# Layer 0's z, q and k products as seven block products for eight, ahead of the SSD branch

## The chip, the core and the metric

One core of a Trainium2 chip runs the whole step. Its engines work side by side, each in the order of its own instructions: PE (TensorE) multiplies and accumulates into PSUM, DVE (VectorE) and ACT (ScalarE) do element work, POOL a little beside them, and SP (SyncE) issues DMAs. They meet at semaphores. The metric is the device time of one execution in microseconds, the median of three runs; smaller is better.

## The reference

One step of a two-layer encoder over 576 tokens (a prompt of 512 and a sample of 64) of width 2048, float32. Layer 0 projects the tokens once and runs two groups of heads on the result, stick-breaking attention (8 pairs of heads) and a Mamba-2 SSD branch (4 groups):

```python
proj = jnp.einsum('bld,de->ble', x, w_in)
q, k, v, g_a, z, xbc, dt_raw = jnp.split(proj, L0_SPLITS, axis=-1)
o_a = stick_breaking(q, k_all, v_all, past).reshape(...) * jax.nn.silu(g_a)
# ssd_branch: xbc through a causal conv of 4 taps and silu -> xs, B, C; a scan by chunks of 64 -> y
y = y.reshape(b_, L, SSD_WIDTH) * jax.nn.silu(z)
yg = yg * lax.rsqrt(jnp.mean(yg * yg, axis=-1, keepdims=True) + RMS_EPS)      # per group
mix = jnp.einsum('ble,ed->bld', jnp.concatenate([o_a, o_b], axis=-1), w_out)
y = layer_norm(DEEPNORM_ALPHA * x + mix, ln_g, ln_b)
```

Stick-breaking weighs key j of query i by exp(log_sigmoid(z_ij) minus the sum of softplus(z_il) over the keys l between them). Layer 1 (chunk-band attention, 16 pairs) is not touched. The change calls layer 0 "layer 1".

## The kernel before

Everything is feature-major: a tile is 128 features by 576 tokens. A float32 operand goes into two float32r parts, `hi` (a copy on ACT) and `lo` (source minus `hi`, on DVE), by `split` (L78 to L86), and a product is three passes: hi by hi, hi by lo, lo by hi. One `product` (L100) gives one tile of 128 outputs: 2 halves of K, 8 slices of K each, 3 passes and 2 halves of 288 tokens, **96 matmuls** of 128x288. A half of K brings 512 KB of weights (`raw`), one `wh` on ACT (L84) and one `wl` on DVE (L85). The result lies in one of the **two** PSUM buffers `pj`; a third product can start when an earlier buffer has been read out.

Layer 0 has 72 such tiles (24 conv tiles, 16 z tiles, and for each of the 8 pairs of stick-breaking heads q, k, v and a gate) and a narrower product for dt. In time:

- x is loaded and split (both parts stay in SBUF), with dt's product and the first conv product as it comes.
- SSD branch, 4 groups. `conv_tile` (L227) makes six tiles of a group (four `xs`, `bT`, `cT`): product, conv on DVE (a multiply-add L239 and three L241), silu. Then small matmuls (transposes `tb` and `tx`, states `pst`, decays `pcb`, outputs `py`), with DVE's element work between them; for each of four tiles a z product (L330), its silu, and z times y; last the norm: `prm` on PE, Ln and Exp on ACT (L374, L375), one L378 for each tile.
- Stick-breaking, 8 pairs. `heads_in` (L418) makes q, k and v with their splits and copies; `run_pairs` (L505) adds the gate's product, for the last four pairs only after all pairs. `sb_attend` works through 8 segments of logits: PE `z`, on ACT Abs, Exp and Ln, on DVE an addition (L561), a scan (L563) and a subtraction (L567), on ACT Exp, PE transposes `tpw`, copies out of PSUM (L464, L466), PE `po` and `pos`.
- `mix_norm`: output projection and layer norm of layer 0; then layer 1.

Products and the small matmuls are interleaved on PE at building time: a product is what PE runs while the other engines work out the operands of the next small matmuls. All DMAs are issued by SP, stores included (`store = nc.sync.dma_start`).

Of the kernel before, what the change touches and what calls it, by code (L numbers as in the profile page):

```python
# [26 lines left out]
NHALF = 3                 # feature tiles of a layer norm's input that go by halves of the tokens  # L27
# [19 lines left out]
def encoder(ctx: ExitStack, tc: tile.TileContext, a):  # L47
# [7 lines left out]
    store = nc.sync.dma_start  # L55
# [22 lines left out]

    def split(pl, src, shape, tag, bufs=None):
# [13 lines left out]
    def parts(cut):  # L93
        """Token slices of the two parts of a product, which meet where two PSUM banks do."""
# [88 lines left out]
    act(dp[0:64], pd[0:64, at], AF.Copy)  # L183
# [44 lines left out]
    def conv_tile(m, tag, bufs):  # L228
        pz = product(a["w_in0"], 48 + m, 2, xh, xl) if m else pconv
# [3 lines left out]
        act(xc[:, 3:515], pz[:, 0:TP], AF.Copy)  # L233
        act(xc[:, 518:582], pz[:, TP:T], AF.Copy)
# [11 lines left out]
    SMP = 515               # column of the first sample token in a conv output  # L246
    for g in range(NG):
# [3 lines left out]
        # token-major x * dt, x * to_end, and B  # L251
# [168 lines left out]
    def heads_in(pe, pl, w, mq, mk, mv, okd, ovd, pr, tiles, flipq=False, ready=None):  # L420
        """Projects q, k, v of a head pair. Returns q and k in parts, feature-major, and v token-major.
        flipq: the queries of the prompt and of the sample in reversed order."""
# [34 lines left out]
        return qs, (qb, *qbs), kh, kl, kf, vt  # L457
# [10 lines left out]
    def transpose_tile(wsrc, r, t, wts, flipq=False):  # L468
        """wsrc [128 queries of tile t of head r, keys] -> wts[block][:, head, queries of t]."""
# [485 lines left out]
```

## Time and profile before

| | |
|---|---|
| median of 3 runs | 2737.75 us (2735.2 to 2739.05) |
| the profiled execution's own span | 2731.6 us |
| PE busy | 2680.1 us, 20126 matmuls |
| DVE busy | 1530.9 us, 2328 instructions |
| ACT busy | 1155.0 us, 1938 instructions |
| moved by DMA | 299.33 MB, mean 110 GB/s |

The span is the time from the first to the last instruction that the profiler saw in one execution; it lies 6.15 us below the median of the runs. A busy share is an average over stages that differ: PE's idle time lies in few places.

### The profile page before, as it was taken

To read this page: it belongs to the slowest core of one execution; us is meant where nothing else is said; L and a number is where in the kernel's file an instruction comes from. 1 tells how busy PE (TensorE), PEld (TensorE's weight loads), DVE (VectorE), ACT (ScalarE), POOL (GpSimd) and SP (SyncE) were. 2 spreads that over 40 slices of the span, in tenths; PEclk is the share of its full clock that TensorE was granted. 3 is DMA by queue.
4 is the path that set the end of the run, shared out by engine and by line. 5 is a ranking of instruction groups with operands and counts; after the bars stand their busy time and mean duration, and the time that the engine had idled before them with its cause. 6 is when DMAs were issued, how large, how long until landed. Compare 5 with 4: busy or idle time off the path is not lost.

```text
span 2731.6 us, 47350 instructions
## 1 busy us (share of the span) xinstructions
PE 2680.1 (98%) x20126; PEld 2577.3 (94%) x20126; DVE 1530.9 (56%) x2328; ACT 1155.0 (42%) x1938; POOL 94.1 (3%) x172
## 2 busy tenths in 40 slices
PE   9999999999999999999998999999999999999996
PEld 8999899999999999999998999999999999999995
DVE  6665657665656767653338545444445555554437
ACT  5434344434555656541225434333334343344224
POOL 0000000000000000000004000000000000000004
PEclk9999999999999999999999999999999999999998
DMA  5222222223232222353235433333333333334334
GB/s 188 78 84 85 66 95 68 93 79 107 91 103 99 92 93 83 109 189 99 95 111 173 142 104 116 110 110 114 114 109 115 109 113 118 114 111 156 104 103 140
DMA packets 111060, 299.33 MB, mean 110 GB/s; under 512 B 12672, under 2 KB 26752, under 8 KB 110848
## 3 DMA queue, kind: packets, MB, share of 16 engines
q1 hardware_dynamic: 110848, 296.30, 32.8%
q8 instruction: 158, 2.59, 0.4%
q14 instruction: 54, 0.44, 0.0%
HBM read 250.82 MB, written 45.42 MB: 108 GB/s over the span
## 4 chain that ended last, share of the span: by engine, by line
PE 95%; DVE 3%; ACT 1%; issue 0%; DMA 0%; SPq 0%; ACTq 0%; DVEq 0%
PE pj L123 79%; PE po L493 3%; PE tpw L473 2%; PE px L123 2%; DVE d L742 1%; PE z L393 1%; PE z L392 1%; PE pos L502 1%; PE z L398 1%; PE pst L287 1%; PE py L356 1%; PE py L358 0%; PE tpw L485 0%; PE tpv L452 0%; PE pcb L338 0%
## 5 line engine op out<-in xcount | busy, mean ns | idle before, releaser
L85 DVE TENSOR_TENSOR wl<-raw,wh 128x1024 fp32r<-128x1024 f32 x367 | 450.6, 1228 | 490.3 <-ACT wh L84 488.3
L84 ACT ACTIVATE wh<-raw 128x1024 fp32r<-128x1024 f32 x367 | 388.3, 1058 | 739.7 <-PE pj L123 632.9
L123 PE MATMUL pj<-yl,wh 128*128 128x288 f32 x2048 | 464.4, 300 | 6.8 <-DVE yl L749 6.8
L123 PE MATMUL pj<-yh,wl 128*128 128x288 f32 x2048 | 455.2, 299 | 0.0
L123 PE MATMUL pj<-yh,wh 128*128 128x288 f32 x2048 | 451.8, 298 | 1.1 <-DVE kf L438 0.9
L123 PEld LDWEIGHTS pj<-yl,wh 128*128 128x128 f32 x2048 | 336.2, 189 | 10.8 <-DVE yl L749 9.0
L123 PEld LDWEIGHTS pj<-yh,wl 128*128 128x128 f32 x2048 | 333.3, 189 | 13.7 <-issue 12.2
L123 PEld LDWEIGHTS pj<-yh,wh 128*128 128x128 f32 x2048 | 336.0, 189 | 5.1 <-issue 2.0
L123 PE MATMUL pj<-oh,wl 128*128 128x288 f32 (+2 forms) x1120 | 254.7, 297 | 3.2 <-DVE wl L85 3.2
L123 PE MATMUL pj<-ol,wh 128*128 128x288 f32 (+2 forms) x1120 | 254.9, 297 | 0.0
L123 PE MATMUL pj<-oh,wh 128*128 128x288 f32 (+2 forms) x1120 | 254.3, 297 | 0.0
L123 PEld LDWEIGHTS pj<-oh,wl 128*128 128x128 f32 x1120 | 186.3, 189 | 3.9 <-DVE wl L85 3.4
L123 PEld LDWEIGHTS pj<-oh,wh 128*128 128x128 f32 x1120 | 186.1, 189 | 0.5
L123 PEld LDWEIGHTS pj<-ol,wh 128*128 128x128 f32 x1120 | 185.8, 189 | 0.3
L741 POOL TENSOR_TENSOR d<-d,mu 128x288 f32<-128x288 f32 (+2 forms) x60 | 60.2, 1038 | 1996.4 <-DVE mu L727 1211.3
L808 ACT ACTIVATE t<-t,smx 128x128 f32<-128x128 f32 (+3 forms) x128 | 71.1, 556 | 83.0 <-DVE smx L806 53.7
L466 ACT ACTIVATE wts<-tpw 128x128 f32<-128x128 f32 (+1 forms) x96 | 41.5, 432 | 127.2 <-PE tpw L473 127.0
L833 DVE TENSOR_TENSOR t<-z,bp 128x128 f32<-128x128 f32 (+3 forms) x128 | 60.5, 485 | 49.8 <-PE tpw L473 46.0
L493 PE MATMUL po<-wts,vt 128*64 128x384 f32 (+3 forms) x384 | 82.6, 442 | 0.0
L464 DVE COPY wts<-tpw 128x128 f32<-128x128 f32 (+1 forms) x96 | 46.7, 487 | 49.7 <-PE tpw L473 48.7
L676 DVE TENSOR_TENSOR d<-xr,pj 128x576 f32<-128x576 f32 (+3 forms) x30 | 20.2, 672 | 88.3 <-PE pj L123 88.3
L453 ACT ACTIVATE vt<-tpv 128x512 f32<-128x512 f32 x24 | 14.2, 594 | 126.4 <-PE tpv L452 126.4
(433 smaller groups left out, 5509.2 us busy)
## 6 DMA issues: line engine op xcount, KB each, us to landing
raw<-w_in SPq DMA_DIRECT2D x272, 512.0 KB, 3.3
raw<-w_out SPq DMA_DIRECT2D x95, 512.0 KB, 3.2
xr<-xT SPq DMA_DIRECT2D x29, 288.0 KB, 5.9
o_scr<-of SPq DMA_DIRECT2D x24, 288.0 KB, 3.0
d<-o_scr SPq DMA_DIRECT2D x24, 288.0 KB, 5.8
o_scr<-z SPq DMA_DIRECT2D x16, 288.0 KB, 2.2
or<-o_scr SPq DMA_DIRECT2D x16, 288.0 KB, 3.3
y_scr<-d SPq DMA_DIRECT2D x16, 288.0 KB, 3.9
```

Of the source, the lines that this page charges most:

```text
L84: act(hi, src, AF.Copy)
L85: tt(lo, src, hi.bitcast(F32), ALU.subtract)
L123: mm(ps[:, at.start + v.start:at.start + v.stop], st[:, c], mv[u * 8 + k][:, v], start=(first and k == 0 and i == 0), stop=(last and k == ...
L287: mm(pst, btok[0:n, c, :], xe[0:n], start=True, stop=True)
L356: mm(o, xdt[:, c, hc], w4[:, r, c, :], start=True, stop=(c == 0))
L464: nc.vector.tensor_copy(dst, src)
L466: act(dst, src, AF.Copy)
L473: nc.tensor.transpose(tp[:, b * P:(b + 1) * P], wsrc[:, b * P:(b + 1) * P], ident)
L493: mm(po[q, b * P:TP], vt[:, b, q], wts[:, b, r, b * P:TP], start=(b == 0), stop=(b == 3))
L741: (tt if tail and m in (0, 1, 2, 3) else nc.gpsimd.tensor_tensor)(r, r, mu[:, v], ALU.subtract)
L808: act(t[:, i, :], t[:, i, :], AF.Exp, bias=sm[:, i:i + 1], accum_out=sm[:, 2 + i:3 + i])
L833: tt(tv[:, i, :], z[:, i * n:i * n + n], bp[seg[i][0]][:, TP - n:TP], ALU.add)
```

## The change

A new function `seven` makes **two** output tiles at once in blocks: the two tiles by the two halves of K give four weight blocks, the two halves of K by the two halves of the tokens four blocks of x. Eight block products of 24 matmuls become seven (Winograd's form of Strassen's scheme): three of them have sums of weight blocks as weights (`s_`, `a21`, made on DVE for each call), three have sums of x blocks (`t57`, `t6`, `t4`, made once by `add_sums`). It is called 16 times ahead of the SSD branch: 8 calls for two z tiles each, 8 for q and k of one pair each. What was made ahead goes to DRAM and comes back where it is used: z after its silu, q and k as `hi` and `lo`, the raw products of the first five conv tiles (`CAHEAD`, made beneath the x sums), and dt. The copy of x whose second token half was replaced by `t4` is restored at the last call. In stick-breaking a pair now only projects v; its gate is deferred for the pairs 3, 5 and 7, not for the last four. `store` is ScalarE's queue for the whole kernel. A pad of SBUF is gone. Layer 1 is the same but for its stores. ACT issues 231 DMAs, before none; SP 769, before 781.

```diff
-    store = nc.sync.dma_start
+    store = nc.scalar.dma_start
+    def add_sums(ya, yb):
+        tt(ya[:, :, H0], ya[:, :, H1], ya[:, :, H0], ALU.subtract)
+        tt(ya[:, :, H1], yb[:, :, H1], ya[:, :, H1], ALU.subtract)
+        tt(yb[:, :, H1], yb[:, :, H1], ya[:, :, H0], ALU.subtract)
+    def block(acc, wt, b, first=True, more=False):
+        wh, wl = split(wpool, wt, [P, 1024], "w")
+        for k, (hi, lo) in enumerate(b):
+            c = slice(k * P, (k + 1) * P)
+            for i, (st, mv) in enumerate(((wh, hi), (wh, lo), (wl, hi))):
+                mm(acc, st[:, c], mv, start=(first and k == 0 and i == 0), stop=(k == 7 and i == 2),
+                   skip_group_check=more)
+    def seven(wa, m0, wb, m1, sums, ps, tmp, last=False):
...
+        block(pa, a11, sums["M1"])
+        act(c11, pa, AF.Copy)
+        block(pb, a12, sums["M2"])
+        tt(c11, c11, pb, ALU.add)
+        tt(s_, a21, a22, ALU.add)
+        block(pc, s_, sums["M5"])
+        act(c22, pc, AF.Copy)
+        tt(s_, s_, a11, ALU.subtract)
+        block(pa, s_, sums["M6"], False, True)
+        act(c12, pa, AF.Copy)
+        tt(a21, a11, a21, ALU.subtract)
+        block(pa, a21, sums["M7"], False, True)
+        tt(c22, c22, pa, ALU.add)
...
+        tt(s_, a12, s_, ALU.subtract)
+        block(pc, s_, sums["M3"], False, True)
+        tt(c12, c12, pc, ALU.add)
+        if not last:
+            block(pa, a22, sums["M4"], False, True)
+            act(c21, pa, AF.Copy)
+        return o0, o1
...
+    for i in range(16):
+        pr, last = i // 2, i == 15
+        if i % 2 == 0:
+            for j, o in enumerate(seven(a["w_in0"], 32 + i, a["w_in0"], 33 + i, sums, ps7, tm7)):
+                silu(tm7, o, o, T, "sl", 1)
+                store(z_scr[i + j], o)
+            continue
+        q, k = seven(a["w_in0"], pr, a["w_in0"], 8 + pr, sums, ps7, tm7, last)
...
     def conv_tile(m, tag, bufs):
-        pz = product(a["w_in0"], 48 + m, 2, xh, xl) if m else pconv
+        early = CORDER.index(m) < CAHEAD
...
         for i in range(4):
-            pz = product(a["w_in0"], 32 + 4 * g + i, 2, xh, xl)
             z = s.tile([P, T], F32, tag="z", name="z", bufs=6)
-            silu(s, pz, z, T, "c1")
+            load(z, z_scr[4 * g + i])
...
-    run_pairs(bl_, NPAIR_SB, 4, sb_heads, sb_attend, a["w_in0"], 24, o_scr0[16:24])
+    run_pairs(bl_, NPAIR_SB, (3, 5, 7), sb_heads, sb_attend, a["w_in0"], 24, o_scr0[16:24])
```

**Start of the SSD branch, DVE.** The rows below are DVE's from the running sum `cum` of dt to the conv of the first tiles (`cy` is a conv's result, `xc` its input, `tp` the transpose on PE of `cum` and dt); first before, then now.

```order
L199 SCALAR_TENSOR_TENSOR cum<-cs_366,dt_a 128x576
L202 TENSOR_TENSOR cumr<-cum,cumr 32x576
L85 TENSOR_TENSOR wl<-raw,wh 128x1024
L212 COPY cumT<-tp 128x128
L213 COPY cumT<-tp 64x32
L239 TENSOR_SCALAR cy<-xc,vec 128x579
L241 SCALAR_TENSOR_TENSOR cy<-xc,vec,cy 128x579 x3
L212 COPY dtT<-tp 128x128
L213 COPY dtT<-tp 64x32
L221 TENSOR_TENSOR te<-pe,cumT 128x128
```

```order
L343 TENSOR_SCALAR dt_a<-dt,ea 128x576
L95 TENSOR_TENSOR wl<-raw,wh 128x1024
L344 SCALAR_TENSOR_TENSOR cum<-cs_4716,dt_a 128x576
L347 TENSOR_TENSOR cumr<-cum,cumr 32x576
L357 COPY cumT<-tp 128x128
L358 COPY cumT<-tp 64x32
L390 TENSOR_SCALAR cy<-xc,vec 128x579
L95 TENSOR_TENSOR wl<-raw,wh 128x1024
L463 TENSOR_TENSOR wS<-pcs,cumT 64x512
L392 SCALAR_TENSOR_TENSOR cy<-xc,vec,cy 128x579
L357 COPY dtT<-tp 128x128
```

Before, one conv tile's product had been done here and the others came in turn. Now the inputs of five tiles come from DRAM, and their conv work stands in one piece behind `cumT` on DVE; the tile `bT`, whose transposes `tb` stand on PE 130 matmuls behind `tp`, is the fifth of them.

**End of the last SSD group, PE.** `py` is the output of the last head, `prm` the sum of squares for the norm, `tpv` the transpose of pair 0's v, `pj` any projection's product; first before, then now.

```order
L123 MATMUL pj<-x2l,wh 128x288 x2
L123 MATMUL pj<-x2h,wl 128x288 x2
L123 MATMUL pj<-x3h,wh 128x288 x2
L123 MATMUL pj<-x3l,wh 128x288 x2
L371 MATMUL prm<-acc,cst 128x288 x2
L123 MATMUL pj<-x3h,wl 128x288 x2
L123 MATMUL pj<-x4h,wh 128x288 x2
L123 MATMUL pj<-x4l,wh 128x288 x2
```

```order
L506 MATMUL py<-wt,xdt 64x128
L508 MATMUL py<-ce,h 64x128
L506 MATMUL py<-wt,xdt 64x128
L508 MATMUL py<-ce,h 64x128
L506 MATMUL py<-wt,xdt 64x128
L508 MATMUL py<-ce,h 64x128
L521 MATMUL prm<-acc,cst 128x288 x2
L606 MATMUL tpv<-cst,vf 128x128 x4
L133 MATMUL pj<-xh,wh 128x288 x2
L133 MATMUL pj<-xl,wh 128x288 x2
```

Before, `prm` stood inside a running projection product; now nothing but the small matmuls stands between the end of the previous product (108 matmuls earlier) and `tpv`.

**End of the last SSD group, DVE.** `acc` is the sum of squares, `vf` the copy of pair 0's v out of `pj`, `st` and `gt` its gate's silu; first before, then now.

```order
L361 SCALAR_TENSOR_TENSOR y_6335<-xs,vec,py 128x512
L363 TENSOR_TENSOR z<-y_6335,z 128x576
L368 TENSOR_TENSOR acc<-acc,y_6335 128x576
L85 TENSOR_TENSOR wl<-raw,wh 128x1024
L378 SCALAR_TENSOR_TENSOR z<-z,vec,rst 128x576 x4
L85 TENSOR_TENSOR wl<-raw,wh 128x1024
L431 SCALAR_TENSOR_TENSOR q_6495<-pj,q_6495 64x512
L438 COPY kf<-pj 128x576
```

```order
L512 SCALAR_TENSOR_TENSOR y_8408<-xs,vec,ys 128x64
L511 SCALAR_TENSOR_TENSOR y_8408<-xs,vec,py 128x512
L513 TENSOR_TENSOR z<-y_8408,z 128x576
L518 TENSOR_TENSOR acc<-acc,y_8408 128x576
L528 SCALAR_TENSOR_TENSOR z<-z,vec,rst 128x576 x4
L601 COPY vf<-pj 128x576
L142 SCALAR_TENSOR_TENSOR st<-pj,st 128x576
L144 TENSOR_TENSOR gt<-pj,st 128x576
L95 TENSOR_TENSOR qbl<-qb,qbh 128x128
```

Before, the splits `wl` of the next products and the reads of `pj` by q and k stood among the norm's instructions; now the reads that free both `pj` buffers, `vf` and `gt`, come after the whole norm.

**Stick-breaking, pair 6, PE.** `z` are logits (`ckh` the cached keys), `tpw`, `tpn` and `tpv` transposes; first a like piece of pair 6 in before, then a piece of pair 6 now.

```order
L398 MATMUL z<-ckh,qbh 128x512
L398 MATMUL z<-ckl,qbh 128x512
L398 MATMUL z<-ckh,qbl 128x512
L123 MATMUL pj<-x2h,wl 128x288 x2
L123 MATMUL pj<-x3h,wh 128x288 x2
L123 MATMUL pj<-x3l,wh 128x288 x2
L452 MATMUL tpv<-cst,vf 128x128 x4
L123 MATMUL pj<-x3h,wl 128x288 x2
L123 MATMUL pj<-x4h,wh 128x288 x2
L123 MATMUL pj<-x4l,wh 128x288 x2
L123 MATMUL pj<-x4h,wl 128x288
L473 MATMUL tpw<-cst,L 128x128
```

```order
L633 MATMUL tpn<-cst,L 64x128
L627 MATMUL tpw<-cst,L 128x128 x4
L542 MATMUL z<-kh_8444,q_11060 128x512
L543 MATMUL z<-kl_8446,q_11060 128x512
L639 MATMUL tpw<-cst,L 128x128 x4
L542 MATMUL z<-kh_8445,q_11067 128x512
L543 MATMUL z<-kl_8447,q_11067 128x512
L639 MATMUL tpw<-cst,L 128x128 x4
L542 MATMUL z<-kh_8444,q_11060 128x384
L543 MATMUL z<-kl_8446,q_11060 128x384
```

Before, projection products stood between the segments; now the whole of pair 6, 140 matmuls, stands without one.

## Rows read from the trace of the kernel before

**Rows 1.** Page, parts 1 and 4: busy times, and shares of the chain that ended last.

```profile
PE 2680.1 (98%) x20126; PEld 2577.3 (94%) x20126; DVE 1530.9 (56%) x2328; ACT 1155.0 (42%) x1938; POOL 94.1 (3%) x172
...
PE 95%; DVE 3%; ACT 1%; issue 0%; DMA 0%; SPq 0%; ACTq 0%; DVEq 0%
```

**Rows 2.** Waits of PE: engine, line waited for: us in total, times, longest us.

```profile
PE pj L123 <- DVE yl L749: 6.8, 6, 1.8
PE cs L725 <- DVE s L682: 6.5, 1, 6.5
PE pj L161 <- DVE wd L157: 6.3, 1, 6.3
PE pj L123 <- DVE kf L438: 4.3, 4, 1.1
PE pj L123 <- DVE wl L85: 3.2, 1, 3.2
```

**Rows 3.** Windows: stretch, length, busy us (count) of PE, PEld, DVE, ACT, POOL; clock, DMA.

```profile
46.00:657.00 611.00, 611.00 (x4607) 578.03 (x4607) 384.40 (x487) 259.38 (x366) 28.04 (x88) 0.99 0.24 79
...
700.00:900.00 200.00, 198.36 (x1521) 189.18 (x1520) 124.51 (x196) 109.81 (x191) 0.00 (x0) 1.00 0.28 93
900.00:1000.00 100.00, 97.57 (x758) 91.97 (x757) 68.34 (x107) 61.95 (x111) 0.00 (x0) 1.00 0.30 100
1000.00:1100.00 100.00, 98.21 (x758) 92.28 (x758) 70.23 (x109) 60.55 (x108) 0.00 (x0) 1.00 0.25 83
...
1200.00:1300.00 100.00, 100.00 (x750) 99.79 (x749) 36.84 (x42) 22.08 (x24) 0.00 (x0) 1.00 0.31 98
...
1420.00:1440.00 20.00, 20.00 (x153) 20.00 (x152) 9.20 (x11) 7.30 (x8) 0.00 (x0) 1.00 0.51 172
1460.00:1480.00 20.00, 14.90 (x89) 14.20 (x88) 18.41 (x32) 15.58 (x32) 6.57 (x6) 0.83 0.58 175
...
2700.00:2715.00 15.00, 6.47 (x32) 4.78 (x30) 13.92 (x23) 9.54 (x18) 10.05 (x11) 0.77 0.34 126
```

**Rows 4.** Instruction groups of DVE, splits and z: busy us, mean ns, idle time ahead.

```profile
L85 DVE TENSOR_TENSOR wl<-raw,wh 128x1024 fp32r<-128x1024 f32 x367 | 450.6, 1228 | 490.3 <-ACT wh L84 488.3
...
L134 DVE TENSOR_TENSOR z<-pj,c 128x576 f32<-128x576 f32 x16 | 12.0, 753 | 3.0 <-ACT c L133 3.0
...
L132 DVE SCALAR_TENSOR_TENSOR c<-pj,c 128x576 f32<-128x576 f32 x16 | 12.0, 750 | 0.0
```

**Rows 5.** The same view, ACT: the split's copy.

```profile
L84 ACT ACTIVATE wh<-raw 128x1024 fp32r<-128x1024 f32 x367 | 388.3, 1058 | 739.7 <-PE pj L123 632.9 <-issue 64.3 <-PE px L123 27.2
```

**Rows 6.** Timeline of SP, 654 to 664 us: one DMA issue.

```profile
655.98 0.33 SPq L90 DMA_DIRECT2D raw<-w_in  x1
```

**Rows 7.** Groups of DVE in the SSD branch and the v copy.

```profile
L241 DVE SCALAR_TENSOR_TENSOR cy<-xc,vec,cy 128x579 f32<-128x579 f32 x72 | 59.1, 821 | 2.4
...
L447 DVE COPY vf<-pj 128x576 f32<-128x576 f32 x24 | 18.2, 759 | 83.7 <-PE pj L123 83.7
...
L239 DVE TENSOR_SCALAR cy<-xc,vec 128x579 f32<-128x579 f32 x24 | 13.8, 575 | 0.0
...
L378 DVE SCALAR_TENSOR_TENSOR z<-z,vec,rst 128x576 f32<-128x576 f32 x16 | 12.0, 814 | 4.2 <-ACT rst L375 4.2
...
L284 DVE TENSOR_TENSOR xdt<-tx,dtT 128x512 f32<-128x512 f32 x16 | 11.0, 686 | 3.3 <-PE tx L281 3.3
```

**Rows 8.** Timeline of PE, 640 to 700 us: start us, us, instruction.

```profile
650.16 0.44 PE L358 MATMUL py<-ce,h 128*64 128x128 f32 x4
...
656.63 1.13 PE L371 MATMUL prm<-acc,cst 128*128 128x288 f32 x4
```

**Rows 9.** Timeline, first and last segment of stick-breaking: start us, us.

```profile
694.80 0.22 PE L392 MATMUL z<-kh,q 128*128 128x128 f32 x1
...
1135.81 0.49 ACT L558 ACTIVATE e<-z 128x384 f32<-128x384 f32 x1
```

**Rows 10.** Group of DVE for the keys' low parts (both layers).

```profile
L444 DVE TENSOR_TENSOR kl<-kf,kh 64x512 fp32r<-64x512 f32 x48 | 32.6, 680 | 2.5 <-ACT kh L442 1.5
```

More of the change, by code (lines that the diff above doesn't have):

```diff
@@ L26 @@
 NEG = -1e30
+CAHEAD = 5
+CORDER = [4 * g + i if i < 4 else 4 * i + g for g in range(4) for i in range(6)]
 NHALF = 3
@@ new lines, in parts_of, with raw, bank @@
+    def parts_of(ts_, v):
+        return [(h[:, v], l[:, v]) for h, l in ts_]
+    def seven(wa, m0, wb, m1, sums, ps, tmp, last=False):
+        def raw(w, m, u, tag, pl, bufs):
+            t = pl.tile([P, 1024], F32, tag=tag, name=tag, bufs=bufs)
+            if w is not None:
+                load(t, w[m, u])
+            return t
+        def bank(tag, bufs=1):
+            return ps.tile([P, 512], F32, tag=tag, name=tag, bufs=bufs)[:, 0:HALF]
+        a11, a21, a22 = raw(wa, m0, 0, "sr", tmp, 4), raw(wb, m1, 0, "sr", tmp, 4), raw(wb, m1, 1, "sr", tmp, 4)
+        s_ = raw(None, 0, 0, "raw", wpool, 2)
+        a12 = raw(wa, m0, 1, "raw", wpool, 2)
+        pa, pb, pc = bank("pa", 2), bank("pb"), bank("pc")
+        o0, o1 = (tmp.tile([P, T], F32, tag="so", name="so", bufs=4) for _ in range(2))
+        c11, c12, c21, c22 = o0[:, H0], o0[:, H1], o1[:, H0], o1[:, H1]
+        if last:
+            block(pb, a22, sums["M4"])
+            act(c21, pb, AF.Copy)
+            pb = bank("pb")
+        block(pa, a11, sums["M1"])
[11 more added lines that the diff above has]
+        tt(c22, c22, pa, ALU.add)
+        if last:
+            tt(c21, c21, pa, ALU.add)
+        tt(s_, a12, s_, ALU.subtract)
[5 more added lines that the diff above has]
+        return o0, o1
@@ L139, in encoder @@
     xp = pool("x0", bufs=1, side="right")
     xq = pool("xr", bufs=8, side="left")
-    xh, xl = [], []
+    xhb, xlb = (xp.tile([P, NK, T], F32R, name=n) for n in ("xh", "xl"))
+    xh, xl = ([t[:, k, :] for k in range(NK)] for t in (xhb, xlb))
     pd, pc0 = (pj.tile([P, 1024], F32, tag="pj", name="pj") for _ in range(2))
@@ L163, in encoder, with aside @@
         terms(pc0, split(wpool, raws[1], [P, 1024], "w"), u, xh, xl, (0, 1), u == 0, u == 1)
-    pconv = pc0[:, at]
     xq.release()
+    tp7 = pool("t7", bufs=1, side="right")
+    st7 = pool("st7", bufs=1, side="left")
+    t4 = st7.tile([P, 8, HALF], F32, name="t4")
+    def aside(dst, src, n=P):
+        t = st7.tile([P, T], F32, tag="ev", name="ev", bufs=3)
+        act(t[0:n], src, AF.Copy)
+        store(dst, t[0:n])
+    aside(d_scr, pd[0:64, at], 64)
+    aside(c_scr[0], pc0[:, at])
@@ new lines, in encoder @@
+    t57, t6 = [], []
+    for k in range(0, 8, 2):
+        ya, yb = (st7.tile([P, 2, T], F32, tag=n, name=n, bufs=2) for n in ("ya", "yb"))
+        load(ya, a["xT"][k:k + 2].rearrange("m p t -> p m t"))
+        load(yb, a["xT"][8 + k:10 + k].rearrange("m p t -> p m t"))
+        add_sums(ya, yb)
+        tt(t4[:, k:k + 2, :], yb[:, :, H0], yb[:, :, H1], ALU.subtract)
+        th, tl = split(tp7, ya, [P, 2, T], f"ta{k}")
+        t57 += [(th[:, i, :], tl[:, i, :]) for i in range(2)]
+        th, tl = split(tp7, yb[:, :, H1], [P, 2, HALF], f"tb{k}")
+        t6 += [(th[:, i, :], tl[:, i, :]) for i in range(2)]
+        aside(c_scr[k // 2 + 1], product(a["w_in0"], 48 + CORDER[k // 2 + 1], 2, xh, xl))
@@ new lines, in encoder @@
+    for k in (0, 4):
+        act(xhb[:, k:k + 4, H1], t4[:, k:k + 4, :], AF.Copy)
+        tt(xlb[:, k:k + 4, H1], t4[:, k:k + 4, :], xhb.bitcast(F32)[:, k:k + 4, H1], ALU.subtract)
+    st7.release()
+    x1, x2 = list(zip(xh[0:8], xl[0:8])), list(zip(xh[8:16], xl[8:16]))
+    sums = {"M1": parts_of(x1, H0), "M2": parts_of(x2, H0), "M3": parts_of(x2, H1), "M4": parts_of(x1, H1),
+            "M5": parts_of(t57, H0), "M7": parts_of(t57, H1), "M6": t6}
+    load(vec, a["vecs"])
+    load(cst, a["consts"])
@@ new lines, in encoder @@
+    ps7 = pool("ps7", bufs=1, space=PSUM)
+    tm7 = pool("tm7", bufs=1, side="left")
+    for i in range(16):
[6 more added lines that the diff above has]
+        q, k = seven(a["w_in0"], pr, a["w_in0"], 8 + pr, sums, ps7, tm7, last)
+        if last:
+            for j in range(8):
+                b = tm7.tile([P, HALF], F32, tag="b", name="b", bufs=3)
+                load(b, a["xT"][j][:, H1])
+                act(xh[j][:, H1], b, AF.Copy)
+                tt(xl[j][:, H1], b, xhb.bitcast(F32)[:, j, H1], ALU.subtract)
+        qh = tm7.tile([P, TP], F32R, tag="qh", name="qh", bufs=1)
+        ql = tm7.tile([P, TP], F32R, tag="ql", name="ql", bufs=1)
+        qk_s = tm7.tile([P, TS], F32, tag="qs", name="qs", bufs=2)
+        act(qh, q[:, 0:TP], AF.Copy, scale=0.125)
+        stt(ql, q[:, 0:TP], 0.125, qh.bitcast(F32), ALU.mult, ALU.subtract)
+        act(qk_s, q[:, TP:T], AF.Copy, scale=0.125)
+        store(q_scr[pr, 0], qh.bitcast(F32))
+        store(q_scr[pr, 1], ql.bitcast(F32))
+        store(s_scr[pr, 0], qk_s)
+        store(a["o_sbk"][pr], k)
+        store(s_scr[pr, 1], k[:, TP:T])
+        for j, t in enumerate(split(tm7, k[:, 0:TP], [P, TP], "k")):
+            store(k_scr[pr, j], t.bitcast(F32))
@@ L232, in conv_tile @@
         nc.gpsimd.tensor_copy(xc[:, 515:518], cs[:, m, :])
-        act(xc[:, 3:515], pz[:, 0:TP], AF.Copy)
-        act(xc[:, 518:582], pz[:, TP:T], AF.Copy)
+        if early:
+            src = c_scr[CORDER.index(m)]
+            load(xc[:, 3:515], src[:, 0:TP])
+            load(xc[:, 518:582], src[:, TP:T])
+        else:
+            pz = product(a["w_in0"], 48 + m, 2, xh, xl)
+            act(xc[:, 3:515], pz[:, 0:TP], AF.Copy)
+            act(xc[:, 518:582], pz[:, TP:T], AF.Copy)
         nc.gpsimd.tensor_copy(cvo[:, m, 0:3], xc[:, 512:515])
@@ L456, in heads_in @@
         act(vt[0:TS, 4, :], tp[0:TS, 0:P], AF.Copy)
[L457 removed]
+        return vt
     flip = [0]
@@ L508, in run_pairs @@
             st = heads(pr)
-            if pr < npair - ndefer:
+            if pr not in late:
                 pg = product(wg, gate0 + pr, 2, xh, xl)
@@ L549, in sb_heads @@
     def sb_heads(pr):
-        return heads_in(be_, b_, a["w_in0"], pr, 8 + pr, 16 + pr, a["o_sbk"], a["o_sbv"], pr, sb_tiles)
+        keys, qb = sb_tiles
+        kh, kl = keys[pr % 2]
+        qs = []
+        for r, q in enumerate(HD):
+            t = b_.tile([P, TP], F32R, tag=f"q{r}", name=f"q{r}")
+            load(t.bitcast(F32)[q], q_scr[pr, 0][q])
+            load(t.bitcast(F32)[HD[1 - r]], q_scr[pr, 1][q])
+            qs.append(t)
+            load(qb[q, q], s_scr[pr, 0][q])
+            load(kh[r].bitcast(F32)[q], k_scr[pr, 0][q])
+            load(kh[r].bitcast(F32)[HD[1 - r]], k_scr[pr, 0][q])
+            load(kl[r].bitcast(F32)[q], k_scr[pr, 1][q])
+        kf = b_.tile([P, TS], F32, tag="kf", name="kf", bufs=2)
+        load(kf, s_scr[pr, 1])
+        return (qs, (qb, *split(b_, qb, [P, P], "qb")), kh, kl, kf,
+                values(be_, b_, a["w_in0"], 16 + pr, a["o_sbv"][pr]))
     def sb_weights(z, n, scans):
```

36 lines of the change are left out of this document (22 added, 14 removed).

## The prediction

> **What bounds the kernel now.** The page's first part says PE is busy 2680.1 of 2731.6 us, and the chain that ended last is 95% PE [rows 1]. So time is gained by taking matmuls from PE and lost wherever PE then waits. The waits of PE show how little it waits: the longest items are 6 to 7 us each, in the layer norms and at the very start, and 4.3 us for the copy of k in the attention layers [rows 2]. The windows show why it waits so little in the stages that the change touches. In the first stretch, which is nearly all of the SSD branch, PE has no idle time and DVE is busy 384.4 of 611 us, that is 63%; in stick-breaking (700 to 1100 us) DVE is busy 263.1 and ACT 232.3 of 400 us, and PE idles 5.9 us [rows 3]. Projection products fill PE while DVE and ACT work out the small matmuls' operands. Behind each product that is taken out of these two stages one must ask what PE runs there instead.
>
> **What it removes.** Sixteen calls of 7 blocks of 24 matmuls stand for 32 products of 96: 2688 for 3072, 384 fewer. In a stretch of nothing but such products 750 matmuls took 100 us, 0.1333 us each [rows 3]. **The saving is 384 x 0.1333 = 51.2 us.** It is certain, since no other matmul is added in a number that counts.
>
> **The blocks themselves.** A block lasts 24 x 0.1333 = 3.2 us on PE and needs one `wl`, 1.23 us on DVE [rows 4], and one `wh`, 1.06 us on ACT [rows 5]. A call lasts 22.4 us. Its DVE work is 7 splits and 4 weight sums of the same size, 11 x 1.23 = 13.5, and some 3 to 4 us of small additions and silu: 17.5 us of 22.4, 78%. One split for 24 matmuls is also the cadence of a product, and 20 us with 153 matmuls show it with DVE at 46% and no idle PE [rows 3]. Two blocks of a call have only the block ahead of them for sum, copy and split in a row (1.23 + 1.06 + 1.23 = 3.5 us against 3.2): at worst 0.5 us each, 16 us over 16 calls; at best nothing, since the sum can start earlier. I take 3 us, near the cadence row. Stores between: one issue took SP 0.33 us [rows 6]; the 7 in a q and k call are 2.3 us on ACT, which has 13 to 15 us of work of its own in a call, nothing on the path.
>
> **Start of the SSD branch.** The five first conv products are done early, but not their conv work, which on DVE stands behind the copy of `tp`. From `tp` to `tb` PE has 130 matmuls left, 17.3 us. In that time DVE must do five convs of 0.58 + 3 x 0.82 + 2 x 0.76 = 4.6 us, 22.8 in all, a sixth without its silu, 3.0, two splits, 2.5, and about 3 us of small instructions and one head's weights [rows 4, 7]: 31 us. `tb` is late by 13 us if consecutive instructions overlap a little (12 to 16). Before, the convs came one for each product of 12.8 us.
>
> **The rest of the branch and its end.** Take from the 611 us of the branch 16 z products (204.8 us) and four early conv products (51.2): 355 us of PE are left. Take from DVE's 384.4 us 40 splits (49.1) and the z tiles' silu, 16 x 1.50 = 24.0 [rows 4]: 311 us. DVE's share goes from 63% to 88%, and at the end there is no cover at all. Behind the last product (pair 0's gate) stand 108 small matmuls, 14 us at 0.13, up to `tpv`. DVE has 53 instructions in that place: 26 of about 0.69 us (17.9), seven of 1.22 (8.5), three of 768 columns at about 0.95 (2.9), seven of 0.76 (5.3), the four norm instructions (3.3), `vf` (0.8) and five of 64 columns (1.2 as an estimate): 39.9 us [rows 4, 7]. 39.9 - 14 = 26 us, in which the next product can't start, since both `pj` buffers wait for `vf` and `gt`. Round trips would add: in the trace the last `py` and `prm` lie 6.5 us apart in the fourth group, with products running beside [rows 8]. Overlap of consecutive instructions takes away as much as 4 us. I take **26 us** (20 to 32). The ends of the three earlier groups keep the next group's conv products as cover; nothing is charged there.
>
> **Stick-breaking.** The eight pairs took 441 us, from the first logits to the last, 55 us a pair [rows 9]; DVE's 263.1 us in 400 [rows 3] are 36 a pair. q and k take four splits (4.9) and about five instructions of 0.7 [rows 4, 10] with them: DVE keeps 28 us a pair. PE keeps 18.6 us of small matmuls a pair (140 at 0.133), 12.8 for v and 12.8 for the gate of five pairs. With v and gate PE has 44 us, with v alone 31: more than 28 on average, but not in order. In pair 6 no product stands among the 140, so PE has 18.6 us against DVE's 28 and the four splits of the next two products (4.9): 33. **14 us lost there, 16 with the round trips** through ACT (13 to 20). At the ends of pairs 4 and 7 stretches of 73 and 56 matmuls without product are 9.7 and 7.5 us; at pair 6's ratio (33 to 18.6) DVE needs 17.2 and 13.3: **7 and 6 us** (8 to 19 together). The 4.3 us that PE waited for `kf` [rows 2] go, and like waits for the loads of q and k come: counted as nothing.
>
> **The output projection's start.** The deferred gates covered the loads and splits of its operands; only the last of three does now. PE waits 3.2 us for a split in before's likeliest such place [rows 2]. I take 4 us (0 to 8).
>
> **Clock.** Where PE is idle for long, the granted clock falls: 0.83 in 1460 to 1480 us, with PE busy 14.9 of 20 us, and 0.77 in 2700 to 2715, with 6.47 of 15 [rows 3]; it goes between the two levels of 1.2 and 2.4 GHz. The four sparse places have 50 us of PE's work, part of it inside waits anyway. I take 4 us (0 to 10). The Trainium skill's page "TensorE: Matmul & The Clock Gate" (section "Loop structure matters more than you think") says that an idle stretch puts the array back to the half rate, and so speaks against taking the fill out; the rows agree. By the page more of the four places' work runs slow than I charge; that is a rival below.
>
> **Transfers.** z, q, k and the conv inputs go to DRAM and come back, in stages whose DMA share is 0.24 to 0.30 [rows 3]; the loads are issued well ahead. The passages into the blocks and out of them, where pools change hands: 2 us (0 to 6).
>
> **Sum.** 3 + 13 + 26 + 16 + 13 + 4 + 4 + 2 = 81 us of losses against 51.2 us: 30 us slower. 2731.6 + 30 = 2762 us of span; the median lies 6.15 us above the profiled span: **2768 us**. With all low bounds (0 + 12 + 20 + 13 + 8 = 53) it is 2 us slower, with all high ones (16 + 16 + 32 + 20 + 19 + 8 + 10 + 6 = 127) 76 us.
>
> **Rivals.** *The chains are shorter than the row sums* (faster). DVE and ACT may have done much of each sparse place ahead, as they are idle 37% and more of these stages now [rows 3], and pair 7's segments can run in pair 6's gap. For it: before, the same instructions cost PE nothing at the end of a group. Against: two of the places hang on PE itself, the tail's transposes come behind the last product, and all that follows hangs on them. The point from which it decides is a loss of 51 us in all; at 20 to 25 us, a third of what I sum for the three stages, the time is about 2709. *ScalarE's queue holds up the splits.* ACT takes 231 DMA issues in its own order, each behind the result that it stores; at 0.33 us [rows 6] they are 76 us of an engine that is idle 58% [rows 1], but a store that waits for DVE's low part stands ahead of the next `wh`, and PE waits. Two us in each call are 32 us more: 2800. The Trainium skill's page "Trainium Kernel Development and Optimization" (section "Key Constraints") says that queues of several engines share the same 16 DMA engines and that issuing from several only saves issue time; SP's issues are not what PE waits for here [rows 2], so there is nothing to gain from the other queue. *The blocks are bound by the splits*: one us for each tight block is the same 32 us, 2800. For it: only 22% of DVE's time is left there; against: the cadence row. *The clock stays low behind the gaps*: half of the four places' 50 us at double time is 25 us in place of 4, 2789; against it, the granted clock of 0.83 above stands in a stretch a quarter idle, and PE's mean there is not yet the lower level.
>
> **How the numbers follow.** The losses named: 0.51; the shorter chains 0.26; ScalarE's queue 0.10; the blocks' splits 0.07; the clock 0.06. The measurement tells differences from about 0.2%, 5.5 us. The first case holds a little chance of no difference (its low bounds) and the second too; slower 0.66, the same 0.09, faster 0.25. The range must reach into the rivals at both ends: 2708 to 2802; the first case alone is 2740 to 2800.
>
> **What would show it.** In the changed profile: fewer matmuls by about 384; windows of the blocks with PE at 97% or more; waits of PE on `bc` at `tb` of about 13 us, on `vf` or `acc` of 20 us and more about the last group's end, and on the weights' chain in pairs 4, 6 and 7; a granted clock under 1 there alone. The prediction is wrong if PE is busy at the group's end, if the blocks show waits on `wl` or `wh` at every call, or if ACT shows idle time ahead of its splits that ends on stores.

## The result, and the profile after

The change takes 2844.13 us, median of four runs (2842.64 to 2845.1), against 2736.47 us for the kernel before beside it: a ratio of 1.0391, interval 1.0376 to 1.0405. It is 108 us slower where 30 were forecast, and outside the range. The sign and the mechanism, lost cover, are those of the forecast; the waits and above all the clock are larger, and the branch's groups lose time where nothing was charged.

The page of the changed kernel, parts 1 and 4 (answers to [rows 1]):

```profile
PE 2679.1 (94%) x19742; PEld 2554.2 (90%) x19742; DVE 1677.9 (59%) x2499; ACT 1211.4 (43%) x2022; POOL 99.3 (3%) x172
...
PE 72%; DVE 6%; ACT 2%; DMA 1%; issue 1%; SPq 0%; ACTq 0%; DVEq 0%
```

The 384 matmuls are gone, yet PE is busy as long as before (2680.1 us): 51.2 us of work went, and 50 came back because the matmuls that are left took longer. The second number is PE's idle time: the span of 2842.4 us less 2679.1 is 163.3 us, before 51.5. The two together are the whole loss: 112 more idle, 1 less busy, 111 us between the two profiled spans. (The medians are 108 apart, since the change's lies only 1.7 us above its profiled span.)

The windows of the changed kernel by stage (columns as in [rows 3]): x and the early products, the blocks, the start of the SSD branch, its groups, its end, stick-breaking, the output projection's start.

```profile
0.00:85.60 85.60, 76.34 (x544) 75.76 (x544) 45.76 (x54) 36.94 (x47) 0.22 (x4) 1.00 0.62 220
85.60:460.00 374.40, 361.89 (x2686) 357.97 (x2687) 259.83 (x277) 191.33 (x270) 0.20 (x2) 1.00 0.43 134
460.00:512.00 52.00, 32.61 (x229) 30.24 (x228) 31.35 (x48) 24.04 (x39) 4.55 (x22) 0.81 0.55 171
512.00:871.00 359.00, 342.34 (x2475) 313.52 (x2474) 261.51 (x347) 147.54 (x220) 30.36 (x73) 0.95 0.25 80
871.00:920.00 49.00, 28.37 (x175) 20.13 (x176) 33.64 (x48) 10.96 (x16) 1.12 (x3) 0.71 0.15 51
920.00:1264.00 344.00, 304.43 (x2223) 269.83 (x2221) 249.68 (x415) 218.13 (x404) 0.59 (x2) 0.92 0.36 114
1264.00:1320.00 56.00, 49.38 (x338) 48.55 (x339) 24.48 (x31) 22.04 (x30) 0.00 (x0) 0.91 0.55 193
```

The reader is to see two things in each row: the stage's length less PE's busy time, which is idle, and PE's busy time for each matmul. Before, the SSD branch took 611.00 us for 4607 matmuls, 0.1326 us each, at a clock of 0.99 [rows 3]. Now the groups take 342.34 for 2475, 0.1383 us, at 0.95; the end 28.37 for 175, 0.162 us, at 0.71. Before's own idle time in stick-breaking is 5.9 us, in this window of the kernel before:

```profile
694.80:1160.00 465.20, 459.33 (x3538) 436.20 (x3537) 306.83 (x477) 275.37 (x484) 0.00 (x0) 1.00 0.29 95
```

The waits of PE behind it (columns as in [rows 2]):

```profile
PE pj L133 <- ACT xc L385: 21.8, 4, 14.4
PE pa L167 <- DVE wl L95: 10.4, 11, 1.6
PE z L542 <- DVE L L735: 9.2, 6, 3.8
PE pcb L488 <- ACT ce L495: 8.9, 4, 3.6
PE pj L133 <- ACT oh L818: 8.6, 3, 4.8
...
PE pst L438 <- DVE xe L435: 6.2, 4, 1.6
...
PE tpv L606 <- DVE vf L601: 5.3, 1, 5.3
```

None of the first five stands among the five of before. The start of the SSD branch on PE's timeline (start us, us, instruction, idle time ahead and what ended it):

```profile
487.20 0.43 PE L133 MATMUL pj<-xh,wl 128*128 128x288 f32 x2
487.56 0.46 PE L356 MATMUL tp<-cst,cum 32*128 32x32 f32 x5
...
491.47 0.72 PE L488 MATMUL pcb<-cumr,selr 64*128 64x512 f32 x2 [1.30 <-ACT wS L464]
495.70 1.22 PE L488 MATMUL pcb<-cumr,selr 64*128 64x512 f32 x2 [3.50 <-ACT ce L495]
511.30 0.85 PE L133 MATMUL pj<-xh,wh 128*128 128x288 f32 x2 [14.38 <-ACT xc L385]
511.94 0.68 PE L133 MATMUL pj<-xl,wh 128*128 128x288 f32 x2
512.42 0.68 PE L133 MATMUL pj<-xh,wl 128*128 128x288 f32 x2
```

Within 24 us PE idles 19.2. What it waits for is `xc`, the copy of a conv product out of PSUM, which frees `pj`. On ACT that copy stands behind silu steps of earlier tiles, and these wait for DVE's convs (for one of them ACT sits idle 4.81 us, until 507.86). After the gap a pair of matmuls starts every 0.48 us, 0.24 us each, where at full clock it is 0.133. The end of the branch, the last outputs `py` to pair 0's v:

```profile
905.27 1.26 PE L506 MATMUL py<-wt,xdt 128*64 128x128 f32 x7 [2.19 <-DVE y L511]
...
912.08 2.05 PE L521 MATMUL prm<-acc,cst 128*128 128x288 f32 x4 [3.20 <-DVE acc L518]
919.47 1.08 PE L606 MATMUL tpv<-cst,vf 128*128 128x128 f32 x4 [5.35 <-DVE vf L601]
```

The order is the one shown ahead of the prediction, `acc`, `prm`, `vf`, with PE behind DVE at every step; between `prm` and `vf` DVE itself waits 3.63 us for the norm's `rst` on ACT.

### The profile page after: what moved, and what is told of

It reads as the page before. It is cut to its first block, busy times and chain, and to the rows that moved or that the text cites. A ratio compares the mean times of both kernels' runs of the same rounds, so it can differ in the third digit from the quotient of the medians.

```text
span 2842.4 us, 47325 instructions
## 1 busy us (share of the span) xinstructions
PE 2679.1 (94%) x19742; PEld 2554.2 (90%) x19742; DVE 1677.9 (59%) x2499; ACT 1211.4 (43%) x2022; POOL 99.3 (3%) x172
## 4 chain that ended last, share of the span: by engine, by line
PE 72%; DVE 6%; ACT 2%; DMA 1%; issue 1%; SPq 0%; ACTq 0%; DVEq 0%
PE pj L133 58%; PE po L647 2%; PE tpw L627 2%; PE px L133 2%; DVE d L910 1%; PE z L542 1%; PE z L543 1%; PE z L548 1%; PE pos L656 1%; PE pst L438 1%; DVE L L731 1%; DVE wl L95 1%; PE py L506 1%; PE tpw L639 0%; PE py L508 0%
## 5 line engine op out<-in xcount | busy, mean ns | idle before, releaser
L133 PEld LDWEIGHTS pj<-yl,wh 128*128 128x128 f32 x2048 | 335.7, 189 | 12.5 <-DVE yl L917 7.9
L133 PE MATMUL pj<-xh,wh 128*128 128x288 f32 x1280 | 290.2, 306 | 24.6 <-ACT xc L385 21.8
L133 PE MATMUL pj<-xh,wl 128*128 128x288 f32 x1280 | 288.9, 304 | 0.0
L133 PE MATMUL pj<-xl,wh 128*128 128x288 f32 x1280 | 288.2, 303 | 0.0
L133 PEld LDWEIGHTS pj<-xh,wh 128*128 128x128 f32 x1280 | 213.6, 194 | 33.8 <-ACT xc L385 23.8
L133 PEld LDWEIGHTS pj<-xh,wl 128*128 128x128 f32 x1280 | 212.9, 193 | 5.0 <-issue 3.9
L133 PEld LDWEIGHTS pj<-xl,wh 128*128 128x128 f32 x1280 | 213.7, 193 | 3.7 <-issue 3.0
```

Of the source, the lines that this page charges most:

```text
L133: mm(ps[:, at.start + v.start:at.start + v.stop], st[:, c], mv[u * 8 + k][:, v], start=(first and k == 0 and i == 0), stop=(last and k == ...
```

## The experiments

Each run was timed beside the kernel before, and the ratios are to that.

**The stores' queue.** One line is undone:

```diff
-    store = nc.scalar.dma_start
+    store = nc.sync.dma_start
```

> The change with one line undone: all stores on SyncE's queue again. Theory (fill): the change loses time because PE has no projection products left to run beside the small matmuls of the SSD branch and of stick-breaking, and runs at the lower clock after the gaps; the queue of the stores has no part in it: 2838 to 2850 us against 2844. Rival (queue): stores that wait for their data in ScalarE's order hold up the splits' copies: at least 20 us faster, under 2824 us.

Measured 2838.11 us, ratio 1.037 (1.0354 to 1.0385). Against the change (1.0391, 1.0376 to 1.0405) the intervals overlap: ScalarE's queue is worth some 6 us, a twentieth of the loss, and that is not clear of noise; that rival falls.

**The z products back in their place**, q and k still by blocks:

```diff
-    for i in range(16):
+    for i in range(1, 16, 2):
...
+            pz = product(a["w_in0"], 32 + 4 * g + i, 2, xh, xl)
             z = s.tile([P, T], F32, tag="z", name="z", bufs=6)
-            load(z, z_scr[4 * g + i])
+            silu(s, pz, z, T, "c1")
```

> The change with the z products back inside the SSD branch as plain products (16 x 96 matmuls); q and k still ahead by eight calls of seven blocks. Theory (fill): the branch gets its fill back, all but the start with its 19 us of waits; 192 matmuls (25.6 us) come back, some 54 us of waits and slow clock go, half of the blocks' stalls (6 us) too: about 2810 us, 2800 to 2820. Rival (the chain of q and k through DRAM is what costs, z costs nothing): 25.6 us slower than the change, 2865 to 2870 us.

Measured 2805.82 us, ratio 1.025 (1.0231 to 1.027): 38 us faster with 192 more matmuls. The branch's groups in this run, and then stick-breaking (windows):

```profile
330.00:880.00 550.00, 548.16 (x4067) 514.24 (x4066) 345.89 (x440) 223.29 (x312) 25.92 (x73) 0.97 0.24 79
900.00:1228.00 328.00, 289.69 (x2091) 252.32 (x2089) 241.39 (x401) 209.11 (x388) 0.00 (x0) 0.91 0.33 109
```

With the fill back PE idles 1.8 of 550 us in the groups, nearly as little as before, and DVE's share is 63% again; the clock there is 0.97 even so. Stick-breaking still loses 38 of 328 us.

**q and k back in their place**, z still by blocks, the last four gates deferred as before:

```diff
-    for i in range(16):
+    for i in range(0, 16, 2):
...
     def sb_heads(pr):
+        return heads_in(be_, b_, a["w_in0"], pr, 8 + pr, 16 + pr, a["o_sbk"], a["o_sbv"], pr, sb_tiles)
...
-    run_pairs(bl_, NPAIR_SB, (3, 5, 7), sb_heads, sb_attend, a["w_in0"], 24, o_scr0[16:24])
+    run_pairs(bl_, NPAIR_SB, range(4, 8), sb_heads, sb_attend, a["w_in0"], 24, o_scr0[16:24])
```

> The change with q and k back inside stick-breaking as before, and the gates of the last four pairs after all pairs as before; z still ahead by eight calls of seven blocks. Theory (fill): stick-breaking and the output projection's start lose their 40 us of waits and 20 us of slow clock, the blocks 6 us of stalls, and 192 matmuls (25.6 us) come back: about 2803 us, 2793 to 2815. Rival (only the SSD branch costs): 2865 to 2870 us.

Measured 2806.17 us, ratio 1.0252 (1.0235 to 1.0269), again 38 us faster. Both halves of the change lose, and about alike. (The gates' places go back with q and k here, so the two are not told apart.)

**The move alone**: plain products in the blocks' place.

```diff
     def seven(wa, m0, wb, m1, sums, ps, tmp, last=False):
...
+        for o, w, m in ((o0, wa, m0), (o1, wb, m1)):
+            act(o, product(w, m, 2, xh, xl), AF.Copy)
         return o0, o1
```

> The change with plain products (8 blocks) in place of the seven, at the same place ahead of the SSD branch and through DRAM as in the change; the sums over x are still made but not used. This is the move alone. Theory (fill): all that is lost is lost by the move; the 384 matmuls come back (51 us) and the blocks' stalls (12 us) go: about 2883 us, 2875 to 2890. Rival (the blocks' own stalls and sums cost as much as they save): about 2844 us, no slower than the change.

Measured 2875.38 us, ratio 1.0504 (1.0488 to 1.0519): 31 us slower than the change, 8 less than expected but clear of the rival. The blocks do save time, 31 of their 51 us, the sums over x not counted, since this run makes them too. All that goes with the move ahead costs 138.

**The start alone**: only the early conv products and dt go through DRAM, z, q, k and the gates are in their old places; the stores stay on ScalarE's queue.

```diff
-    for i in range(16):
...
         early = CORDER.index(m) < CAHEAD
...
+            pz = product(a["w_in0"], 32 + 4 * g + i, 2, xh, xl)
```

> The kernel before in its placement of z, q and k (plain products in their old places, gates as before), with one piece of the change: the first five conv products and dt made first, put to DRAM and read back, stores on ScalarE's queue. The sums over x and the blocks are left out. Theory (fill): the branch's start alone costs what the changed profile shows there, 19 us of waits, about 5 us of slow clock behind them, and 3 us at the passages: about 2764 us, 2755 to 2772. Rival (the start only costs where the rest of the branch has no fill either, since z products would come up into it): 2735 to 2745 us.

Measured 2747.95 us, ratio 1.0049 (1.0033 to 1.0065): 12.5 us, between the two. With z products in the group the early conv tiles cost less than half of what they cost in the change; the start's 19 us are not a property of the start alone.

**Matmuls without use** in the SSD branch:

```diff
+            dw = s.tile([P, P], F32R, tag="dw", name="dw", bufs=1)
+            act(dw, pcb[:, 0:P], AF.Copy)
+            dm = pj.tile([P, 1024], F32, tag="pj", name="dm")
+            for k in range(12):
+                for v in toks:
+                    mm(dm[:, 224 + v.start:224 + v.stop], dw, xh[k % 16][:, v], start=(k == 0), stop=(k == 12 - 1))
```

> The change plus 16 groups of 24 matmuls without use in the SSD branch (one for each head pair of each group, weights a copy of 128 columns of the decays, moved operand x; nothing reads their result): as many matmuls, 384, as the blocks save, 51 us at full clock. They need no split, no load and one small ACT copy each. Theory (fill): most of them run while PE waits, and the granted clock rises over the branch from 0.95: 2835 to 2860 us. Rival (PE's work sets the time there too): 51 us slower, 2890 to 2897 us.

> As the run with 24, with groups of 48: 768 matmuls without use, 102 us at full clock. Theory (fill): the branch has some 57 us of waits and 20 us of slow clock to take them up, not all at the right places: 2870 to 2905 us. Rival (PE's work sets the time): 102 us slower, 2940 to 2948 us.

Measured 2915.71 us (ratio 1.066, 1.0644 to 1.0676) and 2954.64 us (1.0802, 1.0786 to 1.0818): 72 and 111 us slower than the change. The theory as I put it there fails, and so does the rival, which said 51 and 102. By the pages of the first run PE's idle time is 158 us (2912.5 less 2754.5), hardly less than the change's 163, and its busy time has risen by 75 us for 51 us of matmuls. The clock did not rise: from 460 us to the end of the branch it is 0.87 here and 0.91 in the change. The timeline shows one place:

```profile
481.63 1.22 PE L488 MATMUL pcb<-cumr,selr 64*128 64x512 f32 x2 [0.88 <-ACT wS L464]
485.05 6.08 PE L500 MATMUL dm<-xh,dw 128*128 128x288 f32 x24 [2.20 <-ACT dw L496]
491.05 0.73 PE L488 MATMUL pcb<-cumr,selr 64*128 64x512 f32 x2
506.65 0.69 PE L407 MATMUL tb<-cst,bc 128*128 128x128 f32 x2 [14.87 <-DVE bc L144]
...
544.90 3.44 PE L500 MATMUL dm<-xh,dw 128*128 128x288 f32 x24 [0.17 <-ACT dw L496]
```

A group of 24 stands in PE's order ahead of the next head pair's `pcb`, waits itself for its weights `dw`, and takes 6.08 us at the lower clock (a later group takes 3.44). The two `pcb` start 9.4 us apart, in the change 4.2; the wait of 14.87 us behind them is not filled. So idle time of PE isn't room by itself: this fill, ahead of the chain's next step, did not help, where the z products did. That the groups also take a `pj` buffer and change the order of the conv products was not tried apart.

**VectorE work left out**, the same three pieces in the kernel before and in the change:

```diff
-            tt(ce, ce, bcast(cT[:, P:TP], [[0, 2], [1, 384]]), ALU.mult)
...
-                tt(acc, acc, y2, ALU.add)
...
-            stt(zt[i], zt[i], vec[:, V_NW + m:V_NW + m + 1], rst, ALU.mult, ALU.mult)
+            if i == 0:
+                stt(zt[i], zt[i], vec[:, V_NW + m:V_NW + m + 1], rst, ALU.mult, ALU.mult)
```

> The kernel before with some VectorE work of the SSD branch left out: the product of the decays with C (16 instructions of 768 columns), the sum of squares over a group's tiles (12) and the norm's multiplication for three of four tiles (12), 34 us of VectorE by row means. Theory (with the z products in place PE sets the branch's time, VectorE has room): within 4 us of the kernel before. Rival (VectorE's chain sets the time already before): 15 us faster or more.

> The change with the same VectorE work left out as in the run above. Theory (without z products the branch's time is that of the chain PE to VectorE to ACT and back): 15 to 34 us faster than the change, 2810 to 2829 us. Rival (the branch's time is PE's own, or the clock's alone): within 6 us of the change, 2838 to 2850 us.

Measured 2735.27 us in the kernel before, ratio 0.9994 (0.9982 to 1.0006): nothing. In the change 2809.38 us, ratio 1.0269 (1.0245 to 1.0294): 34.8 us faster, just over the top of the 15 to 34 expected. By the pages DVE is busy 29.3 us less (1677.9 to 1648.6), and PE idles 25 us less and is busy 12 us less. The gain comes all along the branch: the branch's first `prm` starts at 586.3 us for 600.0, its last at 877.0 for 913.4. This is the clearest of the runs: the same three pieces of DVE's work are free in the kernel before and on the path in the change. DVE itself is busy 261.51 of 359 us in the change's groups, 73%: what sets the time there is the chain from engine to engine, and not that DVE is full.

**The blocks where there is fill to spare.** In layer 1 of the kernel before PE has no idle time from 1600 to 2400 us while DVE is busy 408 of 800 us. Three versions leave layer 0 as before, and make the gates of eight of layer 1's pairs and v of all 16 (in the third version, of eight) by `seven` ahead of the attention; q and k stay. Two windows of the kernel before, then the first version in the second of them:

```profile
1600.00:2400.00 800.00, 800.00 (x6056) 768.89 (x6055) 407.95 (x779) 312.22 (x622) 0.00 (x0) 1.00 0.35 112
1480.00:1600.00 120.00, 112.12 (x783) 106.62 (x782) 69.22 (x113) 53.54 (x101) 17.64 (x23) 0.94 0.42 140
```

```profile
1480.00:1600.00 120.00, 90.60 (x595) 86.44 (x594) 81.50 (x107) 59.17 (x95) 15.18 (x16) 0.84 0.42 144
```

```diff
+    calls = [("g", i) for i in range(0, 8, 2)] + [("v", i) for i in range(0, 16, 2)]
+    for n, (kind, i) in enumerate(calls):
+        m = (48 if kind == "g" else 32) + i
+        pair = seven(w1, m, w1, m + 1, sums, ps7, tm7, last)
```

> The kernel before with layer 0 untouched, stores on SyncE's queue, and seven blocks for eight in layer 1 (chunk-band attention), where the windows of the kernel before show PE without idle time at DVE 37 to 50 percent: gates of the pairs 0 to 7 and v of all 16 pairs in 12 calls ahead of the attention, gates of the pairs 8 to 11 as plain products beneath the sums over x, all through DRAM. 288 matmuls fewer, 38 us. Theory (fill): q and k stay as fill, so only the blocks' own stalls (12 x 0.9 = 11 us) and 4 us at the passages are lost: about 2714 us, 2705 to 2728. Rival (blocks ahead of their use cost more than they save wherever they stand): 2737 us or more.

> The first run of blocks in layer 1 lost 24 us of waits and some 10 of slow clock in the passage at 1480 to 1600 us, on two places: the plain gate products under the sums were held in PSUM until VectorE's silu, behind its sums; and the first block's weights stood on ACT behind the copies of the x sums. Here the gates go out of PSUM by an ACT copy and get their silu when they are used, and the sums' copies are placed after the first call's third block. v of all pairs and the gates of 0 to 7 in 12 calls as there. Theory: most of that passage's loss goes, 25 of 34 us: about 2728 us, 2718 to 2738. Rival (the loss is spread over the attention, where 1 to 3 percent of PE's time is idle): 2745 us or more.

> As the run b, with v ahead only for every other two pairs (0, 1, 4, 5, 8, 9, 12, 13): 8 calls, 192 matmuls (25.6 us) fewer in all, more fill left in the attention. Theory (what is lost in the attention is lost where fill is thin): 12.8 us of saving less than run b, some 10 us less idle time in the attention: within 6 us of run b. Rival (the attention has fill to spare): 10 to 13 us slower than run b.

Measured 2753.05 us (ratio 1.0063, 1.0048 to 1.0078), 2727.97 us (0.9972, 0.9961 to 0.9983) and 2721.89 us (0.9944, 0.9924 to 0.9965). The first missed its expectation: in the passage between the layer norm and the blocks PE idles 29 of the 120 us from 1480 to 1600, at a clock of 0.84 (before, in the same window, 8 us at 0.94). With the gates copied out of PSUM by ACT and the sums' copies moved behind the third block, 25 us came back. The third, with fewer blocks and more fill, is the fastest kernel of this study, 14 us or 0.56% under the kernel before (0.35 to 0.76%); it was expected within 6 us of the second and is 6 us under it, with intervals that just overlap. Its windows, the passage and the attention:

```profile
1500.00:1600.00 100.00, 86.75 (x587) 83.39 (x588) 71.06 (x90) 45.88 (x71) 8.55 (x9) 0.90 0.50 169
...
1800.00:2400.00 600.00, 600.00 (x4550) 567.58 (x4549) 376.50 (x752) 280.04 (x603) 0.00 (x0) 1.00 0.40 128
```

PE idles nowhere in the attention at DVE 63%, the share that the SSD branch had before [rows 3]. So the scheme that loses 108 us in layer 0 can gain a little where PE has cover to spare. The two are not alike in all else: here it is 8 calls and not 16, and gates and v and not z, q and k; no run moved the same products without the blocks.

## Why the prediction was wrong

The loss splits in two for every run: PE's idle time, and what PE is busy beyond the 2680.1 us of before once the matmuls taken out or put in are counted at 0.1333 us each. Both from the pages of the profiled executions:

| run | span | PE busy | matmuls against before | PE idle | PE busy beyond before's |
|---|---|---|---|---|---|
| before | 2731.6 | 2680.1 | 0 | 51.5 | 0 |
| the start alone | 2745.8 | 2687.7 | 0 | 58.1 | 7.6 |
| z in place | 2807.1 | 2695.7 | -192 | 111.4 | 41.2 |
| q, k in place | 2806.3 | 2683.6 | -192 | 122.7 | 29.1 |
| less DVE, after | 2805.0 | 2667.0 | -384 | 138.0 | 38.1 |
| the change | 2842.4 | 2679.1 | -384 | 163.3 | 50.2 |
| the move alone | 2874.9 | 2739.6 | 0 | 135.3 | 59.5 |
| filler of 24 | 2912.5 | 2754.5 | 0 | 158.0 | 74.4 |

The forecast in these terms was 77 us of waits and 4 of clock less 51 saved, 30; measured are 112 and 50 less 51, 111 between the spans.

**The saving** was right: 384 matmuls, and 31 us of 51 visible in the run of the move alone.

**The waits**: 77 us forecast (the sum without the clock), 112 measured. By stage, with 6.6 us ahead of 46.8 us and 6.8 us up to the projection taken off as before's own: the blocks 12.5 us against 3; the start 19.4 against 13; the groups 16.7 against 0; the end 20.6 against 26; stick-breaking 32.8 against 29; the projection's start 6.6 against 4; passages and the rest 3.5 against 2. The steps that failed here are "I take 3 us, near the cadence row" and "nothing is charged there" for the groups. In the blocks 11 waits for `wl` of up to 1.6 us are the tight blocks that I had bounded at 16 us and set low: a cadence of one split per product's half says nothing of a sum, a copy and a split in a row. In the groups I computed DVE's share of 88% and still charged nothing; the run with less DVE work shows that the branch runs at the chain through DVE throughout, not only at its ends. The start was late for the reason given, DVE's five convs, but the wait came out on `pj`, one step ahead of `tb`. The end came near its 26 us partly by luck: PE's 14 us there counted the 108 instructions, while 0.13 us is the time of one record of the profile, and a plain float32 matmul such as `prm` or `py` leaves two. The window of the end has 175 records, 23 us at 0.1326; the stretch was longer than DVE's 39.9 us too, since the round trips through ACT came on top.

**The clock** is the term that failed outright: "I take 4 us (0 to 10)", measured 50 as the table counts it. (Counted as PE's busy time times the share of the clock not granted, in windows of 1 us, it is 55 us in the change and 13 before.) I looked for it in four sparse places, and it is there, but not at that size. By the windows it is 16 us in stick-breaking (304.43 less 2223 x 0.1298, the rate of 700 to 1100 us in [rows 3]), 5 at the end, 2 at the start and some 4 at the output projection's start, 27 in all: the rival with the clock, 25 us, came near these. Another 14 are in the groups (342.34 less 2475 x 0.1326), where neither it nor I counted any, and some 4 in the blocks; these are 46 of the 50, the rest lies in the mix of shapes.

In the groups the lower clock comes in seven stretches of some 4 to 7 us of PE's work. Four stand behind waits for `xc` (PE starts again at 511.30, 618, 728 and 837 us). Three stand behind the 16 small matmuls `ysp` (sample tokens, 64 columns), with PE busy all the time; the third of them, then one of the run with z in place (windows; the clock is the third number from the end):

```profile
777.00:782.00 5.00, 5.00 (x34) 3.47 (x32) 2.06 (x3) 0.98 (x3) 0.89 (x2) 1.00 0.47 157
783.00:789.00 6.00, 6.00 (x28) 5.25 (x28) 3.25 (x4) 1.44 (x2) 0.00 (x0) 0.50 0.14 46
```

```profile
824.00:832.00 8.00, 8.00 (x35) 6.41 (x34) 3.57 (x5) 1.44 (x2) 0.00 (x0) 0.57 0.10 37
```

With z in place all four groups have such a stretch of 7 us behind `ysp`, 14 us of time by the clock, though PE idles 1.8 of 550 us there; in the kernel before only two groups have one, of 4 us. So only about half of the clock's loss in the groups stands behind waits, and why the stretches behind `ysp` are more and longer than before is open. The table says the same: the two columns do not go together (q, k in place idles more than z in place and has the smaller excess; the filler idles 5 us less than the change and has 24 more). In stick-breaking the low clock stands in three stretches with 19 us of idle time in them (1134 to 1145, 1195 to 1220 and 1243 to 1261 us); no run changed one without the other there.

The Trainium skill's page "TensorE: Matmul & The Clock Gate" (section "A second HAM failure mode: psum-queue depth-cycling") tells of a kernel that idles briefly between groups of matmuls and loses throughput to the clock. The trace agrees in part: in the groups a matmul took 0.1383 us for 0.1326, but three of the seven slow stretches have no idle time ahead of them.

**The rivals.** Shorter chains: no, the waits were longer. ScalarE's queue: some 6 us, not clear of noise. The blocks' splits: 12.5 of the 32 us that it gave, with 11 waits on `wl` in 16 calls, and PE at 96.7% there where the forecast's sign was 97% or more.

## What to carry to other kernels

Work that an engine does while others prepare its next operands is not only cost, it is cover: before moving it away, set the other engines' time in that stage against what is left, and if the shares come near each other (here DVE from 63% to a computed 88%) expect the whole stage, not only its ends, to run at their chain. Charge the clock of TensorE to all matmuls of such a stage, not only to those behind the long gaps: here it cost as much as the blocks saved. A scheme with fewer matmuls belongs where the cover is ample: 16 calls of it lost 108 us in one layer, 8 calls gained 14 in the other.

## What the runs showed of the hardware

A stretch with PE busy 95% of the time (342.34 of 359 us) ran at a granted clock of 0.95 and cost 4% more for each matmul; I had taken such a stretch for full speed. PE need not be idle for the clock to fall: behind the 16 small float32 matmuls `ysp` it was 0.50 from 783 to 789 us with PE busy throughout. The same group of 24 matmuls takes 6.08 us after a gap and 3.44 us otherwise, between the two levels of 1.2 and 2.4 GHz. Plain float32 matmuls leave two records each (`prm` x4 for two instructions), so their time is longer than a count of instructions at 0.133 us gives.
